# Transpositions of the norms share the product banks: two groups of three in a product bank, one in the old bank

## The chip, the cores and the metric

The kernel runs on one core of one Trainium2 chip. The metric is the device time of one execution in microseconds. The profile of one execution gives the span from the first to the last instruction and, for each engine, its instructions in time. The engines are PE (TensorE: matrix products and transpositions), DVE (VectorE), ACT (ScalarE), POOL (GpSimd) and SP (which issues most DMAs).

## The reference, cut to what matters

One transformer block over 1024 tokens of width 1024: a hybrid attention mixer, a cross attention to 256 memory rows, and an MLP with squared ReLU of width 4096. Each of the three stages begins with an RMS norm, and so does the memory:

```python
def _rms_norm(x, g):
    xf = x.astype(jnp.float32)
    y = xf * lax.rsqrt(jnp.mean(xf * xf, axis=-1, keepdims=True) + EPS)
    return (y * g.astype(jnp.float32)).astype(x.dtype)
...
    x = x + _hybrid_mixer(_rms_norm(x, norm1_g[l]), ...)
    x = x + _memory_xattn(_rms_norm(x, norm2_g[l]), mem, mem_norm_g[l], ...)
    x = x + _sq_relu_mlp(_rms_norm(x, norm3_g[l]), w_ff_in[l], w_ff_out[l])
```

Behind each norm stands a product with a weight matrix, which needs the normed rows transposed.

## The kernel before, in words

Tokens are worked in tiles of 128 rows, eight in all. The projections of the first four tiles come first (`project`, pool `p1`). Then two streams run beside each other: the attention of all eight tiles (`attend`), and the fill (`fill`, L1181), a generator that does in turn the projections of tiles 4 to 7 (pool `p2`), the keys and values of the memory (`memory`, L854), `between` for tiles 0 and 1, `between` for 2 and 3, `mlp` for tiles 0 to 3, and `between` for 4 and 5, all in pool `dn`. `together` (L113) mixes the two streams in the program by planned costs. When the attention is done, what is left of the fill is merged with `between` for tiles 6 and 7, which has a pool `d2` of its own (L1209). At the end `mlp_tail` (L1056, pool `d3`) does the MLP of tiles 4 to 7: norms of its first two tiles (the first pair), two groups of features for these, norms of the other two tiles (the second pair), the other groups.

`between` multiplies the attention's output with `w_out`, adds it to the rows, norms them (`norm_T2`), multiplies with `w_xq`, does the cross attention, writes its result to DRAM (`xo_dr`), loads it as `o` (L986 to L988), transposes it and multiplies with `w_xo`.

A norm of a tile in `norm_T2` (L293): ACT squares and sums the row, POOL takes the power -0.5 (`nr`, L234), DVE scales half a row at a time into a `relu` tile (L300, a ring of two), and `to_T` (L271) transposes that half: PE does four transpositions of 128x128 (L277) into one bank of PSUM, and the bank is read by one ACT copy (L281) where the product takes whole fp32 values, or by an ACT copy `xh` (L238) and a DVE subtraction `xl` (L239) where it takes a high and a low part (`mlp` and `mlp_tail`). One such set of four transpositions is called a group below; a tile has two. The bank is free for another group when its last reader is done.

PSUM has eight banks. From the end of `project`'s first part on they are divided by tags:

```python
PSUMS = {"p1": {"D": 4, "M": 3, "C": 1}, "main": {"S": 2, "PT": 2, "PV": 1, "D": 2, "M": 1}}
TAGS = {"p1": ("D", "M", "C"), "p2": ("D", "M", "D"), "dn": ("D", "M"), "d2": ("S", "PT"), "d3": ("D", "M")}
```

A pool's first tag takes its products, its second its transpositions. So in `dn` and `d3` products take turns in two banks D (in the profile psD), and all transpositions share the one bank M (psM). In `d2` products have two banks S and transpositions two banks PT. The attention uses S, PT and PV, never D or M. The products of `gemm` (L303), of `memory_item`, of `mlp` and of `mlp_tail` are made by `mm` (L221); DVE adds them to the rows (L894, in the tail L1126). Weights of the MLP are split into `whi` (L247) and `wlo` (L252).

The program's order gives each instruction its priority; the tile framework then chooses the order on each engine with a simulated timeline (L82), and sets all waits itself.

Of the kernel before, what the change touches and what calls it, by code (L numbers as in the profile page):

```python
# [22 lines left out]
P = 128  # L23
# [22 lines left out]
TAGS = {"p1": ("D", "M", "C"), "p2": ("D", "M", "D"), "dn": ("D", "M"), "d2": ("S", "PT"), "d3": ("D", "M")}  # L46
# [123 lines left out]
def build(nc, tc, I, C, out):  # L170
# [13 lines left out]
    def pst(tag, shape):  # L184
        return psum["pool"].tile(shape, F32, tag=tag, name="ps" + tag, bufs=psum["n"][tag],
                                 padded_shape=[P, 512 // int(np.prod(shape[2:]))] + list(shape[2:]))

    def ring(pool, tag, shape, dt=F32):
        n = RINGS[pool.name if isinstance(pool.name, str) else "dn"][tag]
        return pool.tile(shape, dt, tag=tag, name=tag, bufs=n)  # L190
# [32 lines left out]
    def small(pool, tag, w, dt=F32, bufs=2, p=P):  # L223
        return pool.tile([p, w], dt, tag=tag, name=tag, bufs=bufs)
# [5 lines left out]
    def rsqrt_of(pool, ss, n, w, tag):  # L230
        ms = small(pool, tag + "ms", w)
        v.tensor_scalar(ms, ss, 1.0 / n, EPS, op0=ALU.mult, op1=ALU.add)
        r = small(pool, tag + "r", w)
        g.tensor_tensor(r, ms, mhalf[:, 0:1].to_broadcast([P, w]), op=ALU.pow)  # L234
        return r

    def split_ps(src, hi, lo):
        s.activation(hi, src, AF.Copy)  # L238
        v.tensor_tensor(lo, src, hi, op=ALU.subtract)  # L239
# [28 lines left out]
            nc.sync.dma_start(dst(raw), src)  # L268
        return [raw]

    def to_T(pool, x_t, xs, nk):  # L271

        for c in range(0, nk, 4):
            m = min(4, nk - c)
            pt = pst(TAGS[pool.name][1], [P, m, P])
            for j in range(m):
                te.transpose(pt[:, j, :], x_t[:, (c + j) * P:(c + j + 1) * P], ident)  # L277
            if len(xs) == 2:
                split_ps(pt, xs[0][:, c:c + m, :], xs[1][:, c:c + m, :])
            elif c % 8 == 0:  # L280
                s.activation(xs[0][:, c:c + m, :], pt, AF.Copy)  # L281
            else:
                v.tensor_copy(xs[0][:, c:c + m, :], pt)

    def norm_T(pool, x_t, gb, xs):
        ss = small(pool, "nss", 1)
        xn = ring(pool, "x4", [P, DM])
        s.activation(xn, x_t, AF.Square, accum_out=ss)
        r = rsqrt_of(pool, ss, DM, 1, "n")
        v.scalar_tensor_tensor(xn, x_t, r[:, 0:1], gb, op0=ALU.mult, op1=ALU.mult)  # L290
        to_T(pool, xn, xs, DM // P)

    def norm_T2(pool, x_t, gb, xs):  # L293

        ss = small(pool, "nss", 1)
        s.activation(xs[0], x_t.rearrange("p (k c) -> p k c", c=P), AF.Square, accum_out=ss)
        r = rsqrt_of(pool, ss, DM, 1, "n")
        for c in range(0, DM, 512):
            xn = ring(pool, "relu", [P, 512])
            v.scalar_tensor_tensor(xn, x_t[:, c:c + 512], r[:, 0:1], gb[c // 512], op0=ALU.mult, op1=ALU.mult)  # L300
            to_T(pool, xn, [x[:, c // P:c // P + 4] for x in xs], 4)

    def gemm(pool, xs, nk, nt, wsrc, chunks, consume):  # L303

# [26 lines left out]
    def xT(pool, nt, whole=False):  # L331

        parts = [pool.tile([P, DM // P, nt * P], F32 if whole else F32R, tag="x" + n, name="x" + n)
                 for n in ("h" if whole else "hl")]
        return (parts, [lambda t, k, x=x: x[:, k, t * P:(t + 1) * P] for x in parts],
                lambda t: [x[:, :, t * P:(t + 1) * P] for x in parts])
# [34 lines left out]
    def project(pool, part, pe, st):  # L371
# [36 lines left out]
        def consume(ci, t, pt):  # L408
            T = t0 + t
            if ci in (0, 1):  # L410
                w = 256 if ci == 0 else 128
                gn = cqg if ci == 0 else ckvg
                ss = small(pool, "css", 1)
                raw = ring(pool, "relu", [P, 2, 256])
                s.activation(raw[:, 1, :w], pt[:, :w], AF.Square, accum_out=ss)
                s.activation(raw[:, 0, :w], pt[:, :w], AF.Copy)  # L416
                r = rsqrt_of(pool, ss, w, 1, "c")
                v.scalar_tensor_tensor(raw[:, 1, :w], raw[:, 0, :w], r[:, 0:1], gn, op0=ALU.mult, op1=ALU.mult)
                dst = [c[:, t, :, :] for c in cq] if ci == 0 else [c[:, t:t + 1, :] for c in ckv]
                to_T(pool, raw[:, 1, :], dst, w // P)  # L420
# [433 lines left out]
    def memory(pool):  # L854
# [4 lines left out]
        for t in range(2):  # L859
            x_t = ring(pool, "b4", [P, DM])  # L860
            nc.sync.dma_start(x_t, I["mem"][0, t * P:(t + 1) * P, :])
            norm_T2(pool, x_t, gbm, xt_of(t))
            yield 1.0
# [33 lines left out]
    def between(pool, t0, nt, x2s, keep, res=None):  # L897

        o_of = []
        for t in range(nt):  # L900
            o = ring(pool, "b4", [P, 8, P])
# [9 lines left out]
        _, xf, xt_of = xT(pool, nt, True)  # L911

        gb2 = gain2(pool, W["norm2_g"])
        for t in range(nt):
            norm_T2(pool, x2[t], gb2, xt_of(t))
            yield 1.0
# [68 lines left out]
        for t in range(nt):  # L985
            o = ring(pool, "relu", [P, 512])  # L986
            nc.sync.dma_start(o, xo_dr[t0 + t])
            to_T(pool, o, [x[:, 0:4] for x in xt_of(t)], 4)  # L988
            yield 0.5
        yield from gemm(pool, xf, 4, nt, W["w_xo"], four, add_to)  # L990
        for t in range(nt):
# [5 lines left out]
    def mlp(pool, t0, nt, x2s):  # L997
# [9 lines left out]
        for t in range(nt):  # L1007
            norm_T2(pool, x2[t], gb3, xt_of(t))
            yield 1.0
# [171 lines left out]
    def fill():  # L1181
        for part in range(1, len(PARTS)):
            with tc.tile_pool(name="p2", bufs=1, reuse_waits="tile") as p2:
                yield from project(p2, part, pe, st)
            projected.append(part)
        dn = dn_pool.__enter__()
        yield from memory(dn)
        yield 1, PACES[1]
        yield from between(dn, 0, 2, {}, False)
        yield 3, PACES[2]  # L1190
        x2s = {}
        yield from between(dn, 2, 2, x2s, True)
        yield 3, PACES[3]
        yield from mlp(dn, 0, 4, x2s)
        yield 5, PACES[4]
        yield from between(dn, 4, 2, {}, False)
# [40 lines left out]
```

## Time and profile before

| | |
|---|---|
| time, median of 3 runs | 1802.85 us (1801.54 to 1806.27) |
| the profiled execution | 1801.64 us |
| its span, first to last instruction | 1799.6 us |
| PE busy | 1696.2 us (94%) |
| ACT busy | 1080.4 us (60%) |
| DVE busy | 951.0 us (53%) |
| POOL busy | 892.6 us (50%) |
| mean granted clock of PE | 0.977 |

In the lines below an instruction stands by its start and duration in us, engine, line of the kernel, operation, what it writes and reads (out<-in, buffer numbers left out), shape and count. In square brackets is the time its engine was idle before it, and what ended that wait. The windows view gives for a stretch its length, then the busy time and count of PE, PEld (weight loads), DVE, ACT and POOL, the granted clock of PE as a share of the full one, the share of DMA, and GB/s.

### The profile page before, as it was taken

What the parts mean: (1) busy time and instruction counts of PE and PEld (TensorE: products, weight loads), DVE (VectorE), ACT (ScalarE), POOL (GpSimd) and SP (SyncE); (2) the same over time, 40 slices, a digit from 0 to 9 for tenths busy, and PEclk for the clock granted to TensorE, in tenths of its full rate; (3) what the DMA queues carried; (4) which work ended last, traced back from release to release, by engine and by line L of the source; (5) the groups of instructions that cost most, each with busy time, mean ns of one, the idle gap of its engine ahead of it and who ended that gap; (6) DMA issues with size and microseconds to landing.
All of it is one profiled execution on the core that took longest, in us unless ns stands there. A gap on an engine that the chain in (4) does not pass through costs nothing.

```text
span 1799.6 us, 28055 instructions
## 1 busy us (share of the span) xinstructions
PE 1696.2 (94%) x9326; PEld 1457.3 (81%) x9326; DVE 951.0 (53%) x2381; ACT 1080.4 (60%) x2703; POOL 892.6 (50%) x1025
## 2 busy tenths in 40 slices
PE   5987999899989999999998999999999889999998
PEld 5986888688878777788886888887988878888887
DVE  4555757665873776365654555646524552222223
ACT  4444659797688579856896557994412543333333
POOL 2356647463551355568576576662211444444445
PEclk9997999999999999999999999999989899999999
DMA  6235221366336321222222122225375642333333
GB/s 193 74 119 150 71 76 58 109 197 177 99 107 192 98 63 42 70 71 79 61 67 83 55 71 67 67 75 187 108 245 158 209 118 84 96 94 98 96 118 107
DMA packets 176977, 193.80 MB, mean 108 GB/s; under 512 B 25664, under 2 KB 144192, under 8 KB 176832
## 3 DMA queue, kind: packets, MB, share of 16 engines
q1 hardware_dynamic: 168896, 181.52, 33.2%
q0 software_dynamic: 7936, 10.49, 2.2%
q8 instruction: 74, 1.21, 0.3%
q14 instruction: 71, 0.58, 0.1%
HBM read 170.98 MB, written 20.97 MB: 107 GB/s over the span
## 4 chain that ended last, share of the span: by engine, by line
PE 67%; DVE 9%; POOL 7%; ACT 5%; issue 5%; DMA 5%; SPq 1%; POOLq 0%; ACTq 0%; DVEq 0%
PE psD L221 48%; PE psS L221 8%; PE psPV L221 5%; PE psPT L698 4%; POOL wlo L252 3%; DMA wraw<-in_w_ff_in_dram 1%; PE psM L277 1%; ACT dmask L639 1%; DVE pl L239 1%; DVE S L681 1%; PE psPT L585 1%; ACT S L683 1%; ACT ph L238 1%; DMA qin<-q 1%; ACT whi L247 1%
## 5 line engine op out<-in xcount | busy, mean ns | idle before, releaser
L252 POOL TENSOR_TENSOR wlo<-wraw,whi 128x512 fp32r<-128x512 f32 (+1 forms) x225 | 309.5, 1380 | 266.7 <-ACT whi L247 263.0
L221 PE MATMUL psD<-whi,h 128*128 128x512 f32 x1024 | 340.7, 401 | 9.7 <-DVE b L1126 5.4
L247 ACT ACTIVATE whi<-wraw 128x512 fp32r<-128x512 f32 x321 | 200.7, 628 | 216.7 <-PE psD L221 156.4
L221 PEld LDWEIGHTS psD<-whi,h 128*128 128x128 f32 x1024 | 193.0, 190 | 55.2 <-DVE b L1126 8.8
L221 PE MATMUL psD<-xh,whi 128*128 128x512 f32 (+1 forms) x576 | 212.1, 372 | 1.2 <-ACT xh L238 0.8
L221 PE MATMUL psD<-xh,wlo 128*128 128x512 f32 (+1 forms) x576 | 212.9, 370 | 0.2 <-POOL wlo L252 0.2
L221 PE MATMUL psD<-xl,whi 128*128 128x512 f32 (+1 forms) x576 | 212.1, 370 | 0.0
L221 PE MATMUL psD<-wlo,h 128*128 128x512 f32 x512 | 203.2, 399 | 1.1 <-POOL wlo L252 1.1
L221 PE MATMUL psD<-whi,xh 128*128 128x256 f32 (+1 forms) x704 | 191.7, 353 | 4.3 <-ACT whi L247 3.2
L221 PE MATMUL psD<-wlo,xh 128*128 128x256 f32 (+1 forms) x704 | 191.3, 354 | 1.3 <-DMA wlo<-in_w_in_dram 0.7
L239 DVE TENSOR_TENSOR pl<-psPT,ph 128x512 fp32r<-128x512 f32 (+1 forms) x232 | 142.0, 620 | 80.1 <-ACT ph L238 77.4
L683 ACT ACTIVATE S<-S,mn 128x128 f32<-128x128 f32 (+7 forms) x192 | 142.6, 744 | 38.5 <-DVE mn L681 36.9
L688 POOL TENSOR_SCALAR S<-S,sums,gi 128x640 f32<-128x640 f32 (+7 forms) x128 | 107.0, 846 | 113.7 <-DVE sums L686 101.8
L252 DVE TENSOR_TENSOR wlo<-wraw,whi 128x512 fp32r<-128x512 f32 (+1 forms) x96 | 83.8, 873 | 148.8 <-ACT whi L247 148.5
L238 ACT ACTIVATE ph<-psPT 128x512 fp32r<-128x512 f32 (+1 forms) x232 | 122.7, 539 | 63.2 <-PE psPT L698 59.0
L221 PEld LDWEIGHTS psD<-wlo,xh 128*128 128x128 f32 x704 | 133.3, 194 | 13.4 <-ACT relu L416 1.2
L221 PEld LDWEIGHTS psD<-whi,xh 128*128 128x128 f32 x704 | 130.7, 194 | 14.2 <-ACT whi L247 3.6
L698 PE MATMUL psPT<-c_ident,S 128*128 128x128 f32 x816 | 131.4, 277 | 3.0 <-POOL S L688 1.6
L221 PEld LDWEIGHTS psD<-xh,whi 128*128 128x128 f32 x576 | 108.8, 189 | 19.3 <-ACT xh L238 1.6
L221 PEld LDWEIGHTS psD<-xh,wlo 128*128 128x128 f32 x576 | 109.0, 189 | 17.6 <-POOL wlo L252 0.9
L221 PEld LDWEIGHTS psD<-xl,whi 128*128 128x128 f32 x576 | 108.8, 189 | 17.1
L221 PE MATMUL psS<-K,qh 128*128 128x384 f32 (+3 forms) x288 | 112.7, 395 | 8.6 <-DVE mn L681 4.0
(282 smaller groups left out, 3863.7 us busy)
## 6 DMA issues: line engine op xcount, KB each, us to landing
wraw<-in_w_ff_in_dram SPq DMA_DIRECT2D x40, 512.0 KB, 4.0
wraw<-in_w_ff_out_dram SPq DMA_DIRECT2D x40, 512.0 KB, 3.9
wraw<-in_w_ff_in_dram SPq DMA_DIRECT2D x64, 256.0 KB, 2.7
wraw<-in_w_ff_out_dram SPq DMA_DIRECT2D x64, 256.0 KB, 2.7
whi<-in_w_out_dram SPq DMA_DIRECT2D x32, 256.0 KB, 3.6
wlo<-in_w_out_dram SPq DMA_DIRECT2D x32, 256.0 KB, 3.7
wraw<-in_w_in_dram SPq DMA_DIRECT2D x24, 256.0 KB, 3.7
q<-st SPq DMA_DIRECT2D x12, 512.0 KB, 2.6
```

The source lines that it names most:

```text
L221: te.matmul(o, a, b, start=start, stop=stop)
L238: s.activation(hi, src, AF.Copy)
L239: v.tensor_tensor(lo, src, hi, op=ALU.subtract)
L247: s.activation(hi, raw, AF.Copy)
L252: (v if l == "v" else g).tensor_tensor(lo, raw, hi, op=ALU.subtract)
L277: te.transpose(pt[:, j, :], x_t[:, (c + j) * P:(c + j + 1) * P], ident)
L585: te.transpose(p2[:, h, :], qd[:, h, :, :].rearrange("p b d -> p (b d)"), ident)
L639: s.activation(mask, src, AF.Sign, bias=c, accum_out=over)
L681: v.tensor_tensor_reduce(out=dst, in0=sp, in1=m, scale=1.0, scalar=mn[:, 0:1] if i else 3e38, op0=ALU.add, op1=ALU.min, accum_out=low)
L683: s.activation(S, S, AF.Exp, bias=low, scale=-1.0, accum_out=sums[:, hh:hh + 1])
L688: g.tensor_scalar(Ss[hh], Ss[hh], sums[:, hh:hh + 1], 1.0 if gate is None else gate[:, hh:hh + 1], op0=ALU.mult, op1=ALU.mult)
L698: te.transpose(p2[:, j, hh, :], S[:, (c + j) * P:(c + j + 1) * P], ident)
```

## The change

`to_T` gets an argument `turn`, which only the norms of `norm_T2` and the transposition of `o` in `between` set. A counter runs over all groups of all calls of `to_T`. A group of a call with `turn` goes to the pool's first tag (D in `dn` and `d3`, S in `d2`) unless the counter is a multiple of three, and to the second tag (M, or PT) when it is. Calls without `turn` use the second tag as before.

```diff
-    def to_T(pool, x_t, xs, nk):
+    turns = {"i": 0}
+
+    def to_T(pool, x_t, xs, nk, turn=False):
+
 
         for c in range(0, nk, 4):
             m = min(4, nk - c)
-            pt = pst(TAGS[pool.name][1], [P, m, P])
+            turns["i"] += 1
+            pt = pst(TAGS[pool.name][0 if turn and turns["i"] % 3 else 1], [P, m, P])
             for j in range(m):
                 te.transpose(pt[:, j, :], x_t[:, (c + j) * P:(c + j + 1) * P], ident)
...
             v.scalar_tensor_tensor(xn, x_t[:, c:c + 512], r[:, 0:1], gb[c // 512], op0=ALU.mult, op1=ALU.mult)
-            to_T(pool, xn, [x[:, c // P:c // P + 4] for x in xs], 4)
+            to_T(pool, xn, [x[:, c // P:c // P + 4] for x in xs], 4, True)
...
             nc.sync.dma_start(o, xo_dr[t0 + t])
-            to_T(pool, o, [x[:, 0:4] for x in xt_of(t)], 4)
+            to_T(pool, o, [x[:, 0:4] for x in xt_of(t)], 4, True)
```

## The prediction

> **What bounds the kernel now.** I read the page's first part, then the stages with the view by windows, then the transposition's own groups. The page first.
>
> ```profile
> span 1799.6 us, 28055 instructions
> ...
> PE 1696.2 (94%) x9326; PEld 1457.3 (81%) x9326; DVE 951.0 (53%) x2381; ACT 1080.4 (60%) x2703; POOL 892.6 (50%) x1025
> ```
>
> TensorE (PE) is the bound: busy 1696.2 of 1799.6 us. What the change can give is idle time of PE, or half clock, in the stages where norms are transposed. By windows (stretch, length, busy time of each engine, then the granted clock):
>
> ```profile
> 667.00:693.20 26.20, 21.20 (x129) 16.77 (x128) 24.14 (x70) 25.96 (x69) 12.63 (x16) 0.93 0.05 13
> 693.20:735.00 41.80, 41.80 (x222) 35.11 (x221) 20.76 (x47) 39.28 (x97) 29.09 (x32) 1.00 0.19 61
> 582.00:591.00 9.00, 6.70 (x37) 5.07 (x36) 8.33 (x22) 3.98 (x11) 1.79 (x2) 1.00 0.53 173
> 1310.00:1383.00 73.00, 73.00 (x387) 65.64 (x386) 24.22 (x67) 15.73 (x39) 9.23 (x16) 0.94 0.59 181
> 1392.00:1406.00 14.00, 7.91 (x35) 6.00 (x33) 11.51 (x25) 8.00 (x19) 6.17 (x6) 0.67 1.01 330
> 1406.00:1410.40 4.40, 4.29 (x21) 4.24 (x21) 3.22 (x6) 4.24 (x11) 1.36 (x2) 0.50 0.48 163
> 1464.00:1471.00 7.00, 3.20 (x17) 2.54 (x16) 6.36 (x7) 2.06 (x4) 4.06 (x3) 0.82 0.68 190
> 1471.00:1475.30 4.30, 4.30 (x12) 3.33 (x11) 1.35 (x2) 0.60 (x1) 0.00 (x0) 0.50 0.31 101
> 1482.00:1800.00 318.00, 308.25 (x1434) 254.82 (x1432) 84.89 (x116) 106.73 (x183) 144.35 (x123) 1.00 0.33 100
> ```
>
> Four stages have norms and an idle PE: 582 to 591 (the norms of `between` for tiles 2 and 3, idle 9.00 - 6.70 = 2.30), 667 to 693 (the norms of the fill's `mlp`, idle 5.00, and PE is full right behind them), 1392 to 1406 (the first pair of `mlp_tail`, idle 6.09 and clock 0.67) and 1464 to 1471 (its second pair, idle 3.80, then half clock to 1475.3). Where the last two blocks overlap (1310 to 1383) PE is never idle. From 1482 on the tail is one stream of products at clock 1.00, without norms, so what is won or lost ahead of it stays. Now the transpositions themselves, in the view by lines of 360 to 1490 us:
>
> ```profile
> L277 PE MATMUL psM<-c_ident,relu 128*128 128x128 f32 x184 | 33.7, 302 | 16.0 <-DVE xl L239 4.8 <-DMA relu<-xo 4.4 <-DVE relu L880 3.0
> L277 PE MATMUL psPT<-c_ident,relu 128*128 128x128 f32 x32 | 4.9, 275 | 0.7 <-DVE relu L942 0.7
> ```
>
> Of 16.0 us of idle PE in front of the transpositions into M, only the 4.8 behind `xl` are openly a wait for the bank. A 4.4 behind the DMA of `xo` and a 3.0 behind another operation are no matter of banks. In the block with pool `d2` (psPT, two banks) nothing waits for a bank, and there the other tag, S, has two banks too.
>
> **Which group goes where.** The counter runs over every call of `to_T`, in the order of the program: 16 in each part of `project`, so 32 ahead of `memory`, and 4 + 4 in `memory`. So `memory` has M D D M, the norms of the three `between` of pool `dn` D M D D, M D D M, M D D M, the eight of `mlp` D D M D D M D D, and `mlp_tail` (numbers 89 to 96) D M D D for its first pair and M D D M for its second. Nothing is added to any engine: the same 44 groups of four, the same copies, no DMA. Only which bank a group waits for, and whom it then keeps waiting.
>
> **Part 1: the norms of `mlp`, 667 to 693.**
>
> ```profile
> 667.22 0.60 PE L277 MATMUL psM<-c_ident,relu 128*128 128x128 f32 x4
> ...
> 683.19 0.63 PE L277 MATMUL psM<-c_ident,relu 128*128 128x128 f32 x4 [0.19 <-DVE xl L239]
> ...
> 686.79 0.63 PE L277 MATMUL psM<-c_ident,relu 128*128 128x128 f32 x4 [0.80 <-DVE xl L239]
> ...
> 693.24 0.48 PE L221 MATMUL psD<-xh,whi 128*128 128x512 f32 x1
> ...
> 694.61 0.60 PE L277 MATMUL psM<-c_ident,relu 128*128 128x128 f32 x4
> ```
>
> Eight groups take (694.61 - 667.22) / 7 = 3.9 us each, against 0.6 of transposing, and the first product comes at 693.24, when the seventh is copied. With three banks (D is free here: the product before has been added) the pace is that of ACT and DVE. ACT is what is late next: 25.96 of 26.20 us busy. If the groups came at a third of 3.9, the product would come some 15 us earlier. I take 10, since the copies still queue on that full ACT. PE is idle 5.00 / 26.20 = 19% of the time until then and 0% behind, so 10 x 0.19 = **-2.0** (bounds 0 and -5.0).
>
> **Part 2: `between`, 582 to 591.**
>
> ```profile
> 583.59 0.60 ACT L281 ACTIVATE xh<-psM 128x512 f32<-128x512 f32 x1 [0.57 <-PE psM L277]
> ...
> 584.24 0.66 PE L277 MATMUL psM<-c_ident,relu 128*128 128x128 f32 x4 [0.69 <-ACT xh L281]
> 584.73 1.03 PE L221 MATMUL psD<-whi,xh 128*128 128x256 f32 x4
> ...
> 590.26 0.66 PE L277 MATMUL psM<-c_ident,relu 128*128 128x128 f32 x4 [0.75 <-ACT xh L281]
> ```
>
> PE waits 0.69 and 0.75 for ACT to read M. With another bank the second group runs in that wait, but the product behind needs the first copy, done at 583.59 + 0.60 = 584.19: it can start at about 584.25 instead of 584.73. That is 0.5 twice: **-1.0** (bounds 0 and -1.44). The norms of `memory` and of the other `between` stand among attention work and show no wait of PE for M: 0.
>
> **Part 3: first pair of the tail, 1392 to 1410.**
>
> ```profile
> 1384.85 0.42 DVE L894 TENSOR_TENSOR b<-psD,b 128x256 f32<-128x256 f32 x1 [1.86 <-PE psD L221]
> ...
> 1393.69 0.66 PE L277 MATMUL psM<-c_ident,relu 128*128 128x128 f32 x4 [0.97 <-DVE relu L300]
> ...
> 1395.02 0.44 PE L277 MATMUL psPT<-c_ident,relu 128*128 128x128 f32 x2 [0.66 <-DVE relu L942]
> ...
> 1397.86 1.05 PE L277 MATMUL psM<-c_ident,relu 128*128 128x128 f32 x4
> ...
> 1403.26 0.68 DVE L239 TENSOR_TENSOR xl<-psM,xh 128x512 fp32r<-128x512 f32 x1
> ...
> 1404.08 0.47 PE L967 MATMUL psPT<-c_ident,relu 128*128 128x128 f32 x1 [1.99 <-ACT relu L961]
> ...
> 1404.35 1.06 PE L277 MATMUL psM<-c_ident,relu 128*128 128x128 f32 x4
> ...
> 1406.16 0.58 PE L221 MATMUL psD<-xh,whi 128*128 128x256 f32 x1
> ```
>
> The second group's `xl` ends at 1403.94 and frees M; the third is transposed at 1404.35, and the tail's first product starts at 1406.16. The last product in D before that has been added by 1385.3, so D M D D lets the second group into the 0.66 gap before 1395.02 and the third and fourth in behind their norms. I estimate the first product at about 1401, and it can fill the gap of 1.99. So 0.66 + 1.99, and of the 4.40 us at clock 0.50 that follow, which hold 2.2 us of work, half of the 2.2 lost: 1.1. Sum **-3.8** (bounds 0 and -(6.09 + 2.2) = -8.3).
>
> The Trainium skill, "TensorE: Matmul & The Clock Gate", section "Part 4: PE-mode transpose", says that transposing does not count as work for the clock as other matmuls do. By that the clock would not rise sooner, and this part would be -2.7 instead of -3.8; the 1.05 us of the four transposes at 1397.86, against 0.60 at 667.22, show them inside such a half-clock stretch but not what causes it.
>
> **Part 4: second pair of the tail, 1464 to 1480.**
>
> ```profile
> 1464.17 0.60 PE L277 MATMUL psM<-c_ident,relu 128*128 128x128 f32 x4
> ...
> 1467.45 1.75 DVE L252 TENSOR_TENSOR wlo<-wraw,whi 128x512 fp32r<-128x512 f32 x1
> 1469.12 0.68 DVE L239 TENSOR_TENSOR xl<-psM,xh 128x512 fp32r<-128x512 f32 x1
> 1469.72 1.27 DVE L1126 TENSOR_TENSOR b<-psD,b 128x512 f32<-128x512 f32 x2
> ...
> 1469.95 1.09 PE L277 MATMUL psM<-c_ident,relu 128*128 128x128 f32 x4 [3.80 <-DVE xl L239]
> ...
> 1479.84 0.50 PE L221 MATMUL psD<-xh,whi 128*128 128x512 f32 x1 [0.83 <-ACT xh L238]
> ```
>
> Here is the longest wait for M: PE stands 3.80 us until DVE has copied `xl`. But right behind it DVE adds two products, out of both banks of D. So D was full as well, and a group that by the count goes to D would wait until 1470.4 for the first of them: the stall is not removed, it changes its name. Behind that second group on PE's queue stand the down products, and DVE's additions and the tail's next features wait for them. Groups two and three now hold D, which those products need; one hold is at least ACT's and DVE's copy, some 1.3 us with the 0.68 of `xl`. I take **+0.5** (bounds -(3.80 + 2.15) = -5.9, if DVE's order changes so that stall and half clock both go, and +5.9, if the stall comes a second time).
>
> **Sum:** -2.0 - 1.0 - 3.8 + 0.5 = -6.3. The profiled execution took 1801.64 us (span 1799.6), so 1795.3; against the median of the three runs, 1802.85, it is **1796.5**. What I can't cost: line 82 lets a simulated timeline choose each engine's order, so from 364 us on any neighbours may change places. I count that into the range.
>
> **Rivals.**
>
> *Big gain.* The new order also moves DVE's additions ahead of `xl` at 1469, and the stall of 3.80 with its half clock goes: -6.3 - 0.5 - 5.9 = -12.7, 1790. For it: the 1.75 us of splitting a weight at 1467.45 stand ahead of `xl` and of both additions, and an order could place them otherwise. Against it: nothing in the change moves DVE's queue.
>
> *Banks are not the limit.* The groups come sooner, but ACT (99% busy in 667 to 693) and DVE's order decide when a product starts; 1 us or so is left: 1802.
>
> *Product bank held, slower.* In the tail the copies are late: the second group of the first pair has its `xl` 5.4 us after its transposes began, the first of the second pair 4.95. A D held so long leaves the products with one bank. The first pair then brings 0. In the second pair two products wait, 3.80 + 2.15 for one and 3.80 for the other, +9.75; with -3.0 from parts 1 and 2 that is +6.7, 1809.6. It decides from the point at which those waits exceed the 6.8 us of parts 1 to 3. For it: 1469.72. Against it: no product of the first pair needs D before the groups are copied.
>
> *The clock.* The norms come in a quicker change of short work and short waits, and stages at clock 1.00 (582 to 591) drop too. In 667 to 693 the mean of 0.93 is 0.14 x 26.2 = 3.7 us at half clock, at most 1.85 lost. Seven of these in the four `dn` norm stages and the tail, without a gain, would be +13; half as many, +6.5, gives 1809. Such a loss through cycling among banks is in the Trainium skill, "TensorE: Matmul & The Clock Gate", section "A second HAM failure mode: psum-queue depth-cycling". The 1.00 of 693 to 735, with two banks of D in turn, speaks against it here.
>
> **How the numbers follow.** A measurement of this kernel can tell about 0.3%, 5.4 us, from no change. Forecast 0.44 (0.33 of it faster by more, 0.11 within), big gain 0.15 (faster), no limit 0.10 (within), bank held 0.22 (0.21 slower, 0.01 within), clock 0.09 (slower). Faster 0.48, same 0.22, slower 0.30. Both signs are likely, so the range takes in the means of the outer cases: 1786 to 1810; the forecast's own is 1790 to 1801.
>
> **What would show it.** In the profile after: L277 writes psD and psM; `mlp`'s eight groups lie closer than 3.9 us and the first product comes well ahead of 693; two waits of about 0.7 behind `xh L281` are gone; the tail's first product stands near 1401; the stall near 1466 is still there, now behind `b L1126`. It is wrong if PE's idle time before 1482 grows, or if psD products wait behind `xl L239`.

## The result, and the profile after

The changed kernel takes 1816.95 us (median, 1815.7 to 1819.78), the kernel before beside it 1803.44 us (1801.54 to 1806.27). The ratio is 1.0076, 95% interval 1.0057 to 1.0095: slower by 13.5 us, where 6.3 us less were forecast. The profiled execution took 1817.93 us. The head of its page:

```profile
span 1816.2 us, 28045 instructions
...
PE 1699.0 (94%) x9326; PEld 1456.5 (80%) x9326; DVE 949.0 (52%) x2381; ACT 1083.0 (60%) x2703; POOL 886.5 (49%) x1025
```

The work is the same, 9326 matmuls. What grew is the time in which PE stands: 1816.2 - 1699.0 = 117.2 us against 1799.6 - 1696.2 = 103.4 before, so 13.8 of the 16.6 us of span. The view by windows, before first, says where (the busy time of PE is the second number; lines of `to_T` and behind it stand four further down in all changed kernels, so L277 is now L281, L300 is L304, L1126 is L1130).

```profile
580.00:660.00 80.00, 75.47 (x455) 64.56 (x455) 59.90 (x189) 47.23 (x121) 35.02 (x45) 1.00 0.33 100
660.00:700.00 40.00, 34.21 (x205) 27.73 (x205) 36.17 (x99) 38.67 (x97) 17.07 (x24) 0.96 0.07 21
700.00:800.00 100.00, 96.52 (x461) 77.48 (x460) 46.47 (x96) 75.97 (x178) 66.60 (x62) 1.00 0.24 74
...
1200.00:1300.00 100.00, 97.58 (x566) 85.24 (x565) 63.06 (x156) 53.49 (x111) 27.71 (x30) 1.00 0.43 136
1300.00:1350.00 50.00, 47.82 (x241) 42.31 (x240) 15.40 (x46) 10.49 (x29) 6.43 (x11) 0.90 0.79 244
```

The same stretches of the kernel after:

```profile
580.00:660.00 80.00, 73.37 (x436) 62.45 (x436) 58.02 (x185) 47.97 (x124) 32.14 (x43) 0.98 0.29 89
660.00:700.00 40.00, 35.47 (x207) 30.24 (x206) 31.08 (x79) 38.02 (x91) 19.33 (x23) 0.96 0.11 32
700.00:800.00 100.00, 92.62 (x445) 74.47 (x444) 53.01 (x112) 75.03 (x182) 62.96 (x63) 0.98 0.22 70
...
1200.00:1300.00 100.00, 95.81 (x521) 82.06 (x521) 58.45 (x146) 54.98 (x116) 28.78 (x31) 0.97 0.41 132
1300.00:1350.00 50.00, 41.27 (x240) 35.98 (x239) 21.95 (x61) 18.16 (x44) 9.84 (x15) 0.86 0.58 177
```

Idle PE, after less before: +2.1 us, -1.3, +3.9, +1.8 and +6.5. The stage of the norms of `mlp` (660 to 700) gained, as forecast. The stage behind it lost three times as much. And the largest loss lies at 1300 to 1350, where no norm stands on which the prediction put a term: there the attention ends. Stretches that are not shown have both signs (450 to 500 -1.9, 1350 to 1400 -2.2, 1400 to 1450 +1.9), so from 1300 to 1400 the loss is 4.3 us.

**The norms of `mlp`.** The timeline of PE in after, from the first groups to the first product, and then one row further on:

```profile
668.19 1.18 PE L281 MATMUL psD<-c_ident,relu 128*128 128x128 f32 x8
670.96 0.61 PE L281 MATMUL psM<-c_ident,relu 128*128 128x128 f32 x4
...
681.42 0.60 PE L281 MATMUL psD<-c_ident,relu 128*128 128x128 f32 x4
683.08 0.51 PE L221 MATMUL psD<-xh,whi 128*128 128x512 f32 x1
...
780.84 0.30 PE L221 MATMUL psS<-Kc,qh 128*128 128x64 f32 x1 [2.29 <-ACT ir L611]
```

Eight groups now take (681.42 - 668.19) / 7 = 1.9 us each against 3.9, and the first product comes at 683.08 against 693.24. But ACT is busy 38.02 of the 40 us from 660 to 700, as it was before (38.67). From 700 to 800 PE waits 4.9 us for ACT where it waited 1.6, and the longest of these waits is the 2.29 at 780.84. I read this as products that ran ahead of what ACT can follow, so that the lead is given back.

**The norms of `between`.** The two waits of 0.69 and 0.75 behind ACT's copy are gone. PE transposes the two groups of tile 2 one behind the other and then stands for the next norm, which DVE has not made yet:

```profile
580.10 0.66 PE L281 MATMUL psD<-c_ident,relu 128*128 128x128 f32 x4
...
583.70 1.01 PE L281 MATMUL psD<-c_ident,relu 128*128 128x128 f32 x4 [2.94 <-DVE relu L304]
```

**The end of the attention.** Its last product is the last one into psPV that reads `Vd`. The view by tile of 1290 to 1350 us gives the start of the first and of the last one in that stretch, of before and then of after:

```profile
L221 PE MATMUL psPV<-pl,Vd x16: 276/281/469, 1291.5 to 1304.6; 128*128 128x256 f32 x16
```

```profile
L221 PE MATMUL psPV<-pl,Vd x28: 276/283/468, 1290.1 to 1326.4; 128*128 128x256 f32 x28
```

It comes 21.8 us later. What follows it in after, on PE and then on SP's queue:

```profile
1324.45 1.03 PE L221 MATMUL psD<-whi,xh 128*128 128x256 f32 x4
...
1333.87 0.44 PE L221 MATMUL psD<-h 128*128 128x128 f32 x2 [1.59 <-ACT h L238]
...
1335.24 4.94 PE L221 MATMUL psD<-h 128*128 128x128 f32 x22
...
1344.57 3.78 PE L221 MATMUL psS<-whi,b 128*128 128x256 f32 x8 [4.39 <-DMA whi<-in_w_out_dram]
```

```profile
1327.90 0.59 SPq L716 DMA_DIRECT2D o<-oc  x1
1328.54 12.91 SPq L907 DMA_DIRECT2D b<-o  x16
1341.49 0.43 SPq L268 DMA_DIRECT2D whi<-in_w_out_dram  x1
```

`between` for tiles 6 and 7 needs the attention's last output. SP first writes it out (1327.90), issues 16 loads of it (1328.54, 12.91 us), and only behind these the loads of `w_out`, for which PE waits 4.39 us. The same chain in before, PE and SP:

```profile
1310.14 4.93 PE L221 MATMUL psD<-h 128*128 128x128 f32 x22
1314.88 2.02 PE L221 MATMUL psD<-whi,xh 128*128 128x256 f32 x4
...
1321.78 1.03 PE L221 MATMUL psD<-whi,xh 128*128 128x256 f32 x4
1322.64 1.03 PE L221 MATMUL psS<-whi,b 128*128 128x256 f32 x4
```

```profile
1305.79 0.59 SPq L712 DMA_DIRECT2D o<-oc  x1
1306.42 8.65 SPq L903 DMA_DIRECT2D b<-o  x16
1315.12 0.43 SPq L268 DMA_DIRECT2D whi<-in_w_out_dram  x1
```

Here too the weights come behind the 16 loads, and PE does not stand: from 1314.88 to 1322.64 it has 7.8 us of the fill's products with `w_xq` (psD<-whi,xh) to do. In after such products ran at 1324.45, ahead of the attention's last one, and are missing afterwards.

The 16 loads keep the queue 4.3 us longer in after, but that does not make the chain longer. The first weights behind them land this long after their issue, in before and in after:

```profile
DMA to landing us min/median/max: 7.0/7.0/7.0
```

```profile
DMA to landing us min/median/max: 3.0/3.0/3.0
```

From the write of the attention's last output to the landing of these weights it is 16.3 us in before (1305.79 to 1315.12 + 7.0) and 16.6 in after (1327.90 to 1341.49 + 3.0). The chain is about as long in both. In after PE's other work ends at 1335.24 + 4.94 = 1340.18, and the rest of the chain is the wait.

From the records of PE one can count it: transpositions and products of the fill (psD and psM) that start after 360 us and ahead of the attention's last product are 2660 in before and 2728 in after.

### The profile page after: what moved, and what is told of

Read it like the earlier page. It is cut to its first block, busy times and chain, and to the rows that moved or that the text cites. A ratio compares the mean times of both kernels' runs of the same rounds, so it can differ in the third digit from the quotient of the medians.

```text
span 1816.2 us, 28045 instructions
## 1 busy us (share of the span) xinstructions
PE 1699.0 (94%) x9326; PEld 1456.5 (80%) x9326; DVE 949.0 (52%) x2381; ACT 1083.0 (60%) x2703; POOL 886.5 (49%) x1025
## 4 chain that ended last, share of the span: by engine, by line
PE 44%; DMA 2%; DVE 2%; ACT 1%; issue 1%; POOL 0%; SPq 0%; ACTq 0%; DVEq 0%
PE psD L221 33%; PE psS L221 6%; PE psPV L221 2%; PE psPT L702 2%; DMA whi<-in_w_out_dram 0%; DMA wraw<-in_w_ff_in_dram 0%; DVE b L1130 0%; DMA b<-o 0%; DMA b<-x 0%; SPq L907 0%; DVE wlo L252 0%; ACT whi L247 0%; PE psPT L589 0%; DVE relu L304 0%; POOL wlo L252 0%
## 5 line engine op out<-in xcount | busy, mean ns | idle before, releaser
L252 POOL TENSOR_TENSOR wlo<-wraw,whi 128x512 fp32r<-128x512 f32 (+1 forms) x225 | 305.8, 1364 | 293.1 <-ACT whi L247 281.9
```

The source lines that it names most:

```text
L252: (v if l == "v" else g).tensor_tensor(lo, raw, hi, op=ALU.subtract)
```

## The experiments

The two theories throughout: **held bank** (groups in D keep the products waiting) and **order** (the tags make the simulated timeline choose another order for every engine, and that order is what costs). All ratios are to the kernel before, with a 95% interval.

For the held bank the trace of after can be asked directly. From 360 to 1500 us its waits list no product that stands for the copy of a group (`xh` or `xl`). The only wait for a bank D behind `xl` is that of another group:

```profile
PE psD L281 <- DVE xl L239: 0.2, 1, 0.2
```

This does not rule out that groups in D made the simulated timeline put products later.

**The parts alone.** Each kernel gives only the named call the argument `turn`; the counter runs as in after, so each group has the bank that it has there. In e3 and e4 the transposition of `o` gets the same argument.

```diff
# e1: the tail's eight groups          e2: the fill's mlp
+ norm_T2(pool, x2[t], gb3, xt_of(t), True)
# e3: memory, and between in pool dn   e4: between in pool d2
+ norm_T2(pool, x2[t], gb2, xt_of(t), TAGS[pool.name][0] == "D")   # e4: == "S"
```

> Only the eight groups of the tail's norms take turns (D M D D and M D D M); all others stay in the old bank. Theory A, attention ends late: the loss of 13.5 us comes from the stretch in which the fill runs beside the attention, where the fill's norms let its products go ahead and the attention's last output comes 22 us later (1305.8 us before, 1327.9 us after); the tail alone is then harmless, 1799 to 1805 us, and the last oc stands at 1306 as before. Theory B, product bank held: in the tail nothing covers a product that waits for a bank; most of the loss is here, 1810 us or more. Theory C, any new order: the time of the parts has nothing to do with that of the whole; anything from 1795 to 1815.

> Only the eight groups of the norms of the fill's mlp take turns (D D M D D M D D). Theory A: the first product of mlp comes some 10 us earlier, as after the whole change, the attention's outputs are 5 to 15 us late from there on, and the time is 1808 to 1820 us. Theory B: the fill's products wait for D only here, and attention covers it: 1800 to 1806. Theory C: anything from 1795 to 1815, and not in step with the attention's end.

> Only the groups of memory and of the three between of pool dn take turns, norms and the transposition of o; mlp, tail and the last between (pool d2) stay as before. Theory A: a part of the loss, in step with how much later the attention's last output comes: 1803 to 1812 us. Theory B: 1800 to 1806. Theory C: anything from 1795 to 1815.

> Only the groups of the last between (pool d2) take turns, in the banks S of its products and its old banks PT, of which there are two each. Theories A and B: the same as before within 0.3%, since no group waited for PT and the attention has ended. Theory C: anything from 1795 to 1815.

| kernel | us | ratio |
|---|---|---|
| e1, tail | 1806.49 | 1.0019 (1.0006 to 1.0031) |
| e2, mlp | 1806.97 | 1.0014 (1.0003 to 1.0026) |
| e3, memory and between in dn | 1811.01 | 1.0042 (1.0026 to 1.0059) |
| e4, between in d2 | 1803.99 | 1.0005 (0.9994 to 1.0016) |

No part is a gain, and together they make 0.0080, near the 0.0076 of the whole. That adding up is a coincidence, as the later kernels show. e1 is a little over the time that was called harmless, and e2 is under the 1808 to 1820 that its late attention was to cost: its attention's last product, at 1310.9, is no later than in kernels with before's order (up to 1310.7, see the end). In e2 the give-back is plain; its timeline has the wait of 780.84 at 5.70 us:

```profile
782.51 0.42 PE L221 MATMUL psS<-Kc,qh 128*128 128x64 f32 x1 [5.70 <-ACT ir L611]
```

In e1 the second pair of the tail shows the wait under its new name, PE first and then DVE:

```profile
1476.84 0.79 PE L221 MATMUL psD<-whi,h 128*128 128x512 f32 x1 [4.52 <-DVE b L1130]
```

```profile
1471.56 3.42 DVE L304 SCALAR_TENSOR_TENSOR relu<-b,nr,g 128x512 f32<-128x512 f32 x2 [0.63 <-POOL h L1114]
...
1475.51 0.68 DVE L239 TENSOR_TENSOR xl<-psM,xh 128x512 fp32r<-128x512 f32 x1
1476.11 1.27 DVE L1130 TENSOR_TENSOR b<-psD,b 128x512 f32<-128x512 f32 x2
```

DVE scales two norms (3.42 us), then copies `xl`, then adds the two products that keep D; PE stands 4.52 us where it stood 3.80 before. But it is a product that stands there, and what keeps D is earlier products whose additions come late. The pair's two groups for D come only behind that wait:

```profile
1484.79 0.60 PE L281 MATMUL psD<-c_ident,relu 128*128 128x128 f32 x4
1485.73 0.66 PE L281 MATMUL psD<-c_ident,relu 128*128 128x128 f32 x4 [0.35 <-DVE b L1130]
```

A wait of this kind needs no group in D: g1 (below), whose tail has before's banks, has one of 3.38 us behind the same addition, at 1487.01.

**The tail taken apart.** f3 gives `turn` to the first pair alone; f4 to all eight groups, and takes the attention's old bank PV, which is free in the tail, in place of D, for every second group.

```diff
# f3
+ norm_T2(pool, x2[t], gb3, xt_of(t), t < 2)
# f4 (tail only)
+ pt = pst("PV" if turn and turns["i"] % 2 else TAGS[pool.name][1], [P, m, P])
```

> Only the groups of the tail's first pair take turns (D M D D); the second pair and all else stay in M. The whole tail in turn cost 3.4 us, and in its trace the first pair's product came earlier while the second pair stood 4.52 us behind an addition out of D and transposed two groups late. If that is the price, this kernel is at or under the one before: 1799 to 1804. If it is the first pair that costs, 1806 to 1808.

> All eight groups of the tail take turns between M and the bank PV, which the attention has left; no group takes a bank of a product. If holding D was what cost 3.4 us in the tail, this is at or under the kernel before, 1798 to 1804, and the wait near 1466 is left, since there both banks of D wait for their additions. If a quicker order of norms costs by itself, 1806 to 1809.

f3: 1803.03 us, 0.9995 (0.9986 to 1.0005). f4: 1799.89 us, 0.9969 (0.9954 to 0.9984). So the first pair brings nothing that can be told, the second pair in D costs 0.0019 + 0.0005 = 0.0024 or 4.3 us (each with an interval of about 0.001 either way), and the eight groups gain when four of them are in a bank that no product uses. The wait near 1466, which was expected to stay in f4, is gone: the longest from 1450 to 1500 is 1.09 us. The stretch of 1450 to 1500 us, e1 and then f4:

```profile
1450.00:1500.00 50.00, 43.43 (x224) 36.50 (x224) 22.12 (x28) 19.25 (x37) 20.65 (x21) 0.90 0.34 106
```

```profile
1450.00:1500.00 50.00, 47.76 (x253) 40.44 (x252) 18.69 (x27) 22.80 (x44) 26.53 (x26) 0.97 0.41 119
```

PE is busy 4.3 us longer in it and at a higher clock (e1's profile is of an execution of 1811.40 us, 4.9 above its median). So in the tail the choice of the bank decides. That groups in D keep products waiting is not shown: in e1 the products wait for late additions, and DVE's order there is another than in f4.

**The pace.** f1 is after, f2 before, with a planner's number that was to let the fill run slower beside the attention in its last part.

```diff
-PACES = (1.35, 1.35, 1.35, 1.75, 1.75)
+PACES = (1.35, 1.35, 1.35, 1.75, 1.4)
```

> The whole change, with the planner's last pace lowered from 1.75 to 1.4, so that the fill's last between is let in later beside the attention. Theory A, attention ends late: in the whole change 9 us of the 13.5 are lost between 1300 and 1350 us, where the attention's last output is 16 us later than in a run of the old order and little of the fill is left to cover the load of it. With the lower pace the attention ends at least 8 us earlier than 1327.9, PE's idle time of 8.5 us in 1310 to 1360 falls under 4, and the time is 1805 to 1812 us. Rival, the loss lies in the norms and in the banks themselves: no change, 1814 to 1820.

> The kernel before with the same lower pace, as the control of the run of the whole change with that pace. Theory A: nothing to win, since the attention ended in time and enough of the fill was left; 1800 to 1808. Rival, that the pace is simply better by itself: 1795 or less.

f1: 1815.82 us, 1.0062 (1.0047 to 1.0077); f2: 1804.46 us, 1.0004 (0.9994 to 1.0013). It was meant to bring the attention's end forward in f1, and did not: the last product stands at 1327.9, and 2728 of the fill are ahead of it as in after. The edit did not reach the order: in the traces f2 has before's order on every engine to the end, and f1 has after's until 1370. So the two are repetitions of before and, up to there, of after, and tell nothing of the cause.

**Another order without another bank.** h1 and h2 leave every bank as before and add one tiny instruction to the norms of pool `dn`.

```diff
# h1, ahead of the first group of each norm
+ v.memset(small(pool, "dum", 1), 0.0)
# h2, ahead of the second group of each norm
+ s.activation(small(pool, "dum", 1), mhalf, AF.Copy)
```

> All banks as before; one VectorE memset of one element per partition is put ahead of the first group of each norm of the blocks with pool dn (ten memsets, together under 2 us of VectorE, which is 53% busy). It changes the order that the simulated timeline chooses about as much as the change does (5437 lines of TensorE's list differ, against 6676). If the change's price is the new order as such, whichever it is, this kernel moves by several tenths of a per cent either way: ratio outside 0.998 to 1.002. If the price is the product bank that the groups hold, it stays at 1.000 within 0.001, 1801 to 1806 us, and the attention ends near 1306 to 1312.

> As the other control, with a ScalarE copy of one element per partition ahead of the second group of each norm of the dn blocks: another order of the engines (1849 lines of TensorE's list differ from before), all banks as before. New order as such: outside 0.998 to 1.002. Held bank: within 0.001 of before.

h1: 1799.79 us, 0.9983 (0.9968 to 0.9997). h2: 1810.62 us, 1.0051 (1.0032 to 1.0069). h1 lies between the bounds of the two theories (0.001 and 0.002); h2 is far outside. In the traces all twelve added instructions run early, from 353 to 364 us, and take 12 x 0.06 us of DVE in h1 and 12 x 0.19 = 2.3 us of ACT in h2, a quarter of the 9.2 us that h2 loses. Without a single bank changed the time moves by +0.5%, two thirds of what the change cost. The theory of the held bank does not give that.

**The same change, other groups.** g1 is the change in all of pool `dn`, with d2 and the tail as before. g4 is after with the counter advanced by one.

```diff
# g4
-            pt = pst(TAGS[pool.name][0 if turn and turns["i"] % 3 else 1], [P, m, P])
+            pt = pst(TAGS[pool.name][0 if turn and (turns["i"] + 1) % 3 else 1], [P, m, P])
```

> The change in all blocks of pool dn (memory, the three between, mlp), old bank in d2 and in the tail. If the parts add, as e2 and e3 suggest: ratio 1.0014 + 0.0042 = 1.0056, 1813.5 us. If the late end of the attention in the kernel after (1327.5 us against 1306 to 1314 in the parts) comes only where the parts meet, it shows here as well, last product of the attention near 1327, and the ratio is 1.006 or more; if the tail or d2 is needed for it, the attention ends near 1314.

> The kernel after with its counter advanced by one: still two groups of three in the product bank in all blocks, but other groups (mlp M D D M D D M D, tail's pairs M D D M and D D M D). If holding a product bank is what costs, whichever group does it: ratio 1.005 to 1.009 as after. If the price is one particular meeting in the order, it moves by more than 0.003 from after's 1.0076, and the attention's end moves with it by 5 us or more from 1327.

g1: 1819.48 us, 1.0099 (1.0076 to 1.0121). g4: 1800.60 us, 0.9988 (0.9976 to 1.0). (In g4's trace the groups of `mlp` go D M D D M D D M, not as its expectation spells them.) g4 also puts about two groups of three into D, and it is not slower than before at all. Held banks as such do not cost 0.76%. A part of g4's speed is the clock: its PE is busy 1690.9 us with the products for which before needs 1696.2, at a granted clock of 0.983 against 0.977, and idle 106.2 us against 103.4. By idle time alone g4 loses 2.8 us where after loses 13.8; whether its order brings the higher clock is open. g1 is 0.0043 above the sum of e2 and e3, and its attention ends late too: what the late end needs comes about in the fill, without d2 or the tail. (Like f1 it has after's order on every engine until 1370.)

**The late end by itself.** j1 has before's banks and lets the fill run ahead in `mlp`; j2 and j3 are after with the eight groups of `mlp` moved by one or by two in the count, five of them in D either way.

```diff
# j1
-PACES = (1.35, 1.35, 1.35, 1.75, 1.75)
+PACES = (1.35, 1.35, 1.35, 2.0, 1.75)
# j2: mlp's calls with (turns["i"] + 1) % 3: D M D D M D D M
# j3: mlp's calls with (turns["i"] + 2) % 3: M D D M D D M D
```

> Before's banks, the fill let run further ahead of the attention (PACES[3] 1.75 to 2.0): in TensorE's list 3442 matmuls of the fill stand ahead of the attention's last product, against 3408 in before and 3445 in after. If after's late end of the attention and its idle stretch at 1300 to 1360 come from having too little of the fill left, they come here too without any bank changed: last product of the attention at 1320 or later, idle TensorE of 1300 to 1360 at 6 to 9 us (before 2.2, after 8.7), ratio 1.003 to 1.006. If they come from held banks: idle 2 to 3 us there and a ratio within 0.0015 of 1.

> After, but the eight groups of mlp go D M D D M D D M (five in D, against six); all others as in after. The list still puts 3445 matmuls of the fill ahead of the attention's last product. Theory of the order: as after, ratio 1.006 to 1.009, idle of 1300 to 1360 about 8.5 us, attention's last product at 1325 or later. Theory of held banks: five for six groups, a little under after, and equal to the kernel with M D D M D D M D.

> After, but the eight groups of mlp go M D D M D D M D (five in D as well); all others as in after. Here the list puts 3416 matmuls of the fill ahead of the attention's last product, as in the kernel that had only mlp in turn. Theory of the order: idle of 1300 to 1360 about 4 us, attention's last product at 1318 or earlier, and a ratio at least 0.002 below that of the kernel with D M D D M D D M. Theory of held banks: the same ratio as that one within 0.0015.

j1: 1808.63 us, 1.0033 (1.0018 to 1.0049). j2: 1812.35 us, 1.0054 (1.0036 to 1.0072). j3: 1804.94 us, 1.001 (1.0001 to 1.002). The windows of the three, in that order:

```profile
1300.00:1350.00 50.00, 43.59 (x232) 38.37 (x232) 17.02 (x45) 13.76 (x33) 7.90 (x12) 0.83 0.63 194
```

```profile
1300.00:1350.00 50.00, 42.95 (x231) 37.06 (x229) 18.30 (x51) 14.78 (x38) 7.89 (x12) 0.83 0.66 203
```

```profile
1300.00:1350.00 50.00, 46.42 (x267) 40.42 (x266) 19.43 (x53) 14.15 (x37) 8.66 (x13) 0.97 0.75 231
```

Idle 6.4, 7.1 and 3.6 us. So the late end comes with before's banks as soon as the fill is ahead, and mostly goes with after's banks when it is not. j1 and j2 fall somewhat short of what the order was to give (a last product at 1320 and 1325 or later, for j2 a ratio of 1.006 to 1.009). Held banks would make j2 and j3 equal within 0.0015; they differ by 0.0044. In j1 PE stands for another transfer on the same queue, the load of `xo`, which SP issues among the 16 loads:

```profile
1332.37 1.09 PE L281 MATMUL psM<-c_ident,relu 128*128 128x128 f32 x4 [3.49 <-DMA relu<-xo]
```

All kernels by the count in their traces (the expectations count in the list of the compiled order, and have other numbers):

| kernel | fill ahead of the attention's last product | that product, us | PE idle 1300 to 1350, us | ratio |
|---|---|---|---|---|
| before | 2660 | 1304.6 | 2.2 | 1 |
| f2 / f3 | 2660 | 1305.1 / 1307.8 | 2.4 / 3.0 | 1.0004 / 0.9995 |
| e1 / e4 / f4 | 2660 | 1310.4 / 1310.7 / 1309.8 | 2.4 / 2.4 / 2.4 | 1.0019 / 1.0005 / 0.9969 |
| h1 / g4 | 2660 | 1300.4 / 1300.3 | 2.4 / 2.4 | 0.9983 / 0.9988 |
| j4 | 2660 | 1297.2 | 1.3 | 0.9936 |
| e3 / h2 | 2660 | 1313.0 / 1316.2 | 2.2 / 2.4 | 1.0042 / 1.0051 |
| e2 | 2668 | 1310.9 | 4.2 | 1.0014 |
| j3 | 2684 | 1313.8 | 3.6 | 1.0010 |
| after / g1 / f1 | 2728 | 1326.4 / 1324.7 / 1327.9 | 8.7 / 8.4 / 8.5 | 1.0076 / 1.0099 / 1.0062 |
| j2 | 2728 | 1320.1 | 7.1 | 1.0054 |
| j1 | 2740 | 1318.4 | 6.4 | 1.0033 |

At a count of 2660 PE is idle 1.3 to 3.0 us there, a little above it 3.6 and 4.2, from 2728 on 6.4 to 8.7, whichever banks the groups have. The ratio follows the count only in part: e3 and h2 lose 0.4 to 0.5% with the count of before.

**The two cheapest together.** j4 takes the fill and d2 of g4 and the tail of f4.

```diff
# turn is 2 in the fill and d2, 9 in the tail
+ pt = pst("PV" if turn == 9 and turns["i"] % 2 else
+          TAGS[pool.name][0 if turn and turn < 9 and (turns["i"] + turn - 1) % 3 else 1], [P, m, P])
```

> The two cheapest together: the fill and d2 with the counter advanced by one (as in g4, 0.9988 with its tail in D), and the tail's groups between PV and M (f4, 0.9969). 3408 matmuls of the fill stand ahead of the attention's last product. If the two are independent: 0.994 to 0.997, 1792 to 1798 us, faster than every kernel so far. If the gain of either was one of order alone and does not carry over: 0.998 or more.

j4: 1791.70 us, 0.9936 (0.9921 to 0.9951), faster than before and after. It differs from g4 only in the banks of the tail's groups (PV and M in turn, for D and M), and by 0.0052; f4 differs from e1 in the same way, by 0.0050. In the tail it is the bank that counts, in either order of the fill. Against g4 6.2 of the 8.6 us of span are idle time of PE; against before only 3.4 of 11.1, and 7.7 are busy time (1688.5 against 1696.2), at the clock of g4 (0.983). What the fill's new order gives in g4 (0.9988, with a tail in D) is one draw among orders, as h1 is.

## Why the prediction was wrong

**The step that failed is the sum, with the sentence that ends it**: the four terms were taken from before's order, and that "line 82 lets a simulated timeline choose each engine's order" was counted into the range. The new order was not a margin on the terms but the main effect: with no bank changed it is worth -0.17% and +0.51% (h1, h2), and between two phases of the same change 0.88% (after, g4). Forecast was 1796.5, within 1786 to 1810; measured were 1816.95. The sentence "any neighbours may change places" was too small as well: not neighbours, but 68 products and transpositions of the fill were moved ahead of the attention's end. At 1310 to 1383 the prediction read "PE is never idle" and put no term there; after has 8.7 us of idle PE in 1300 to 1350, because what filled the wait for SP's loads was work that a new order can spend earlier. Of the prediction's two signs of being wrong the first came, more idle PE. The second did not: no product waits behind `xl`.

**Part 1 (-2.0).** The first product was estimated 10 us earlier and came 10.2 us earlier. The step from there to a gain failed. The 1.3 us of idle PE saved by 700 are lost by 800 (+3.9), behind an ACT that was, as the prediction saw, "what is late next". e2 measures the whole of it at +0.14% or 2.5 us.

**Part 2 (-1.0).** Both waits went, and 2.94 us behind DVE's norm came; 580 to 660 has 2.1 us more idle PE. The 0 for `memory` and the other `between` was the worse step: e3 costs 0.42%, and e3 keeps count and idle time at 1300 of before, so its price (in its profile 5.7 us more idle and 3.5 us more busy PE) lies in yet another part of the order, which no run here has named.

**Part 3 (-3.8).** It came to 0 (f3, 0.9995), and the tail's first product, estimated at about 1401, starts at 1408.83 in after. The groups do come earlier, but the tail's first product does not stand behind them. In f3 the last group begins at 1402.88, and PE then waits 2.44 us for an ACT operation of d2's cross attention, with the first product right behind that:

```profile
1408.11 0.48 PE L971 MATMUL psPT<-c_ident,relu 128*128 128x128 f32 x1 [2.44 <-ACT relu L965]
1408.23 0.56 PE L221 MATMUL psD<-xh,whi 128*128 128x256 f32 x1
```

The prediction wanted to fill that gap (1.99 in before) with this product; on PE's queue it stands behind the wait.

**Part 4 (+0.5).** The mechanism came only in e1, and there by half: a stall stays under the name of `b` (4.52 behind L1130), but a product stands in it, not a group. In after it is absent; the longest wait among the second pair's groups there is that of the last one, for M:

```profile
1494.86 0.78 PE L281 MATMUL psM<-c_ident,relu 128*128 128x128 f32 x4 [2.37 <-DVE xl L239]
```

That the second pair alone costs 4.3 us, within the bounds of -5.9 to +5.9, is so in part luck. The rival "product bank held" priced the two waits at 9.75 us.

**The rivals.** That one had the sign, and in e1 the place, but not the mechanism, since no product of after waits for the copy of a group. It does not give the loss either: in g1, with the tail as before, the kernel is no faster than after. "The clock" falls for after: the mean granted clock of the profiled execution is 0.978 against 0.977. "Big gain" and "banks are not the limit" fall with the result; but the ground given against the first, that nothing moves DVE's queue, was wrong, since DVE's order is another than before's from 1404 us on in e1 and from 1403 on in f4. No rival named the order.

The Trainium skill, "Perfetto Trace Analysis", section "Matmuls", asks that independent groups rotate through different banks, so that the copy of one lies beside the work of the next. The traces agree where the other bank is free (f4, 0.9969) and differ where products need it (e1, 1.0019).

**Open.** Why the timeline takes 68 instructions of the fill ahead of the attention's end in after and none in g4; what h1 gains and h2 and e3 lose before 1300 us; and how much of the 0.76% beyond the 6.5 us at 1300 to 1350 belongs to any one place. The stretches above sum to 13 of the 13.8 us of added idle time; that is by place, not by cause, and the gains and losses of the other stretches nearly cancel.

## What to carry to other kernels

Where a scheduler with a simulated timeline orders the engines, an edit of a buffer's tag is an edit of the whole order behind it: before believing a change of half a per cent, run one or two controls that change the order and nothing else, and look in the trace whether they did change it. Rotate transpositions into a bank that nothing else needs at that time, not into a bank of the products (0.9969 against 1.0019 in this tail). And read a stage in which PE is never idle for what fills it: work that may run earlier is cover that can be spent.

## What the runs showed of the hardware that was not expected

The 16 loads of `o` keep SP's queue for 12.91 us in after and 8.65 us in before, the same loads of the same size; j3's took 7.64. The weights behind them are issued later by as much, but after the longer time they land sooner (3.0 us after the issue, against 7.0), so a queue that is kept longer did not here mean a longer way. No run tells what sets either time.

Kernels that have before's order on every engine until the attention's end (before, f2, f3, f4, e1, e4) have its last product at 1304.6, 1305.1, 1307.8, 1309.8, 1310.4 and 1310.7 us in their profiles. One profile can stand 6 us off another of the same order by then, which is as much as most terms of the prediction's sum. f2, which keeps that order to the end, has 105.9 us of idle PE against 103.4 in before.
